# Seven block products at three instead of two of the eight k-tile pairs of each wide FFN panel

## The chip, the cores and the metric

One core of a Trainium2 chip runs the whole program. The metric is the device time of one execution in microseconds (us); of the kernel before, the median of three executions is shown. The engines have names of their own in the rows: PE is TensorE (PEld its weight loads), DVE is VectorE, ACT is ScalarE, POOL is GpSimd, SP is SyncE, which issues the weight loads from memory.

## What is computed

Two transformer-like layers over 256 tokens of width 2048, in float32. Each ends in a feed-forward network (FFN) of width 8192, and only that part is touched:

```python
u = rmsnorm(x, g_mlp) @ w_up                        # 256x2048 @ 2048x8192
return x + jnp.square(jax.nn.relu(u)) @ w_down      # 256x8192 @ 8192x2048
```

The second layer has the same FFN with other weights. All other parts (state space mixer, sparse attention, delta rule) stay as they are.

## The kernel before

**Precision.** Every float32 operand is split in two parts of a shorter format, `hi` (ScalarE, a copy into fp32r) and `lo` (VectorE, operand minus `hi`). A product is three TensorE passes: hi by hi, lo by hi and hi by lo. An activation tile of 128 by 128 is the stationary operand, 512 columns of weights stream past it; each such pass is one matmul instruction at L250.

**Panels.** `ffn` (L369) takes the hidden width in four slices of 2048. A slice has two wide panels up (`up0`, `up1`; 1024 columns of `w_up` each) and two down (`down0`, `down1`; 1024 columns of `w_down` each), so an FFN is the sequence up0, up1, down0, down1, four times. The very last down panel of an FFN goes by the older function `panel` (L192 to L194) instead. There are thus 15 wide panels in each FFN and 30 in all.

**A wide panel** (`wide`, L235) goes over 2048 rows of weights in eight pairs j = 0..7 of k-tiles. For each pair SyncE loads 1 MB into a `wst` buffer (L267; three such buffers). The result is 256 tokens by 1024 columns: four blocks in four PSUM banks.
- An ordinary pair makes two weight halves of 1024 columns with `parts` (`whi` L261 on ScalarE, `wlo` L262 on VectorE) and uses each in 12 matmuls: 24 matmuls.
- At the pairs in `SPAIRS` the 2 by 2 blocks of tokens/k against k/columns are multiplied with seven products instead of eight (P1 to P7, 21 matmuls). For that VectorE makes sums and differences of weight blocks, `t13` (L279, 1024 columns) and `t24` (L282 and L283, 512 columns each), and the splits need seven blocks of 512 columns instead of four: three halves of 1024 and one of 512. P1, P5, P6 and P7 have banks of their own, so a panel holds all eight banks of PSUM.
- `shared` (L302 on) adds the four extra banks up when the panel's last such pair is through: a ScalarE copy (L306) and four VectorE additions (L307 to L310).

**The activation side.** For every pair in `SPAIRS` the activations must also exist as four sums and differences, split in two parts (`sfh`, `sfl`). `a_forms` (L224) makes them: four VectorE operations on 128 columns (L227 to L230) and one split (ScalarE 512 columns, VectorE 512 columns). For the up panels this is done once per FFN in `x_to_act` (L339); for the down panels once per slice in the end of each up panel (L386 on).

**The end of an up panel.** Four additions on VectorE (L376), ReLU and square on ScalarE (L377, L378), then 16 transposes on TensorE (L390) into PSUM banks that the panel has left, then the splits (L170 ScalarE, L172 VectorE) into the tiles `hT`. For a pair in `SPAIRS` the transposed block is first copied to a buffer `ff` (L394) from which both the split and the forms are made. With `SPAIRS = (2, 5)` pair 2 comes from the end of up0 and pair 5 from the end of up1. The end of a down panel is eight additions into the residual (L410, L413).

**Buffers and order.** The tile framework orders the instructions of each engine when the program is built, by the order of the program and by what its own model holds ready, and each engine then runs its list strictly in order. `whi` and `wlo` have four buffers each, so the splits can be four halves ahead of TensorE. The pool `s2` has 16 buffers of 2 KB, `s4` has 17 of 4 KB, of which 8 hold the input of the FFN and 8 the `hT` tiles of the running slice.

Of the kernel before, what the change touches and what calls it, by code (L numbers as in the profile page):

```python
# [12 lines left out]
AF = mybir.ActivationFunctionType  # L13
# [44 lines left out]
def build(ctx, tc, I, out, tap=None, upto=99):  # L58
    nc = tc.nc
    V, S, G, PE = nc.vector, nc.scalar, nc.gpsimd, nc.tensor  # L60
# [17 lines left out]
    def s4(shape, dt=F32, name="s4"):  # L78
        return sb.tile(shape, dt, name=name, tag="s4", bufs=N4)

    def s2(shape, dt=F32, name="s2"):
        return sb.tile(shape, dt, name=name, tag="s2", bufs=N2)
# [7 lines left out]
    def psum(kind, shape):  # L90
        return pp.tile(shape, F32, name=kind, bufs=2)
# [77 lines left out]
    def split(ps, hi, lo, gain=None):  # L169
        S.activation(hi, ps, AF.Copy, scale=1.0 if gain is None else gain)  # L170
        if gain is None:
            V.tensor_tensor(lo, ps, hi.bitcast(F32), op=OP.subtract)  # L172
        else:
            V.scalar_tensor_tensor(lo, ps, gain, hi.bitcast(F32), op0=OP.mult, op1=OP.subtract)

    def quarter(name):
        return s4([128, 4, 256], F32R, name + "h"), s4([128, 4, 256], F32R, name + "l")

    def at_k(act):
        return lambda kt: tuple(a[:, kt % 4, :] for a in act[kt // 4])  # L180
# [37 lines left out]
            mms(*m)  # L218
        return ps

    SPAIRS = (2, 5)
    turn = [0]

    def a_forms(f, forms, j):  # L224

        sf = s2([128, 4, 128], name="sf")
        V.tensor_tensor(sf[:, 0], f[:, 0, 1], f[:, 1, 1], op=OP.add)  # L227
        V.tensor_tensor(sf[:, 2], f[:, 0, 0], f[:, 0, 1], op=OP.subtract)
        V.tensor_tensor(sf[:, 1], sf[:, 0], f[:, 0, 0], op=OP.subtract)
        V.tensor_tensor(sf[:, 3], f[:, 1, 0], sf[:, 1], op=OP.subtract)  # L230
        sh, sl = s2([128, 4, 128], F32R, "sfh"), s2([128, 4, 128], F32R, "sfl")
        split(flat(sf), flat(sh), flat(sl))
        forms[j] = sh, sl

    def wide(w, r0, c0, lhs, forms):  # L235
# [5 lines left out]
        for k, names in zip((ka[0], ka[1], kb[0], kb[1]), (("P2", "P3"), ("P4", "E"), ("P1", "P5"), ("P6", "P7"))):  # L241
            for b in names:
                B[b] = psum(k, [128, 512])
        ns = len(SPAIRS)
        left = {b: 3 * ns + (0 if b in ("P1", "P5", "P6", "P7") else 6 * (8 - ns)) for b in B}
# [19 lines left out]
        for j in range(8):  # L265
            s = stp.tile([128, 2048], F32, name="wst")
            nc.sync.dma_start(s.rearrange("p (k n) -> p k n", k=2),  # L267
                              w[r0 + j * 256:r0 + j * 256 + 256, c0:c0 + 1024].rearrange("(k p) n -> p k n", p=128))
            if j not in SPAIRS:
                for kk in range(2):  # L270
# [68 lines left out]
    def x_to_act(x, q, gain, forms=None, p=0):  # L339

        for k0 in range(0, 4, 2):
            ps = psum("tp", [128, 512]).rearrange("p (k t c) -> p k t c", k=2, t=2)
            for kk in range(2):
                for t in range(2):
                    PE.transpose(ps[:, kk, t, :], x[:, t, (k0 + kk) * 128:(k0 + kk + 1) * 128], ident)  # L345
            if forms is not None and 2 * p + k0 // 2 in SPAIRS:
                f = s2([128, 2, 2, 128], name="ff")
                for kk in range(2):
                    S.activation(f[:, kk], ps[:, kk], AF.Copy, scale=gain[:, k0 + kk:k0 + kk + 1])
                f_to_act(f, q, k0, forms, 2 * p + k0 // 2)  # L350
                continue
            for kk in range(2):
                k = k0 + kk
                split(ps[:, kk].rearrange("p t c -> p (t c)"), q[0][:, k], q[1][:, k], gain[:, k:k + 1])

    def f_to_act(f, q, k0, forms, j):
        fv = f.rearrange("p k t c -> p (k t c)")
        split(fv, flat(q[0][:, k0:k0 + 2]), flat(q[1][:, k0:k0 + 2]))
        a_forms(f, forms, j)

# [5 lines left out]
    def flat(ap):  # L366
        return ap.rearrange("p k c -> p (k c)")

    def ffn(X, act, forms, w_up, w_down, r, after, tail=0):  # L369
        for s_ in range(4):  # L370
            hT, hforms = [], {}
            for P in range(2):
                B, tags = wide(w_up, 0, s_ * 2048 + P * 1024, at_k(act), forms)
                us = {}
                for i, l, part, bank in shared(B):
                    V.tensor_tensor(part, bank, part, op=OP.add)  # L376
                    S.activation(part, part, AF.Relu, scale=r[:, i:i + 1])  # L377
                    S.activation(part, part, AF.Square)  # L378
                    us[i, l] = part
                for l in (1, 0):  # L380
                    q = quarter("hT")
                    p = len(hT)
                    hT.append(q)
                    for k0 in range(0, 4, 2):
                        pt = psum(tags[k0 // 2], [128, 512])
                        pv = pt.rearrange("p (k t c) -> p k t c", k=2, t=2)  # L386
                        for kk in range(2):
                            for t in range(2):
                                c = (k0 + kk) * 128
                                PE.transpose(pv[:, kk, t, :], us[t, l][:, c:c + 128], ident)  # L390
                        j = 2 * p + k0 // 2
                        if j in SPAIRS:
                            f = s2([128, 2, 2, 128], name="ff")
                            S.activation(f.rearrange("p k t c -> p (k t c)"), pt, AF.Copy)  # L394
                            f_to_act(f, q, k0, hforms, j)
                        else:
                            split(pt, flat(q[0][:, k0:k0 + 2]), flat(q[1][:, k0:k0 + 2]))
            for P in range(2):
                if (s_, P) == (3, 1):
                    for p in (2, 3):  # L400
                        ps = panel(w_down, s_ * 2048, 16, p * 512, 512, at_k(hT), tail=tail if p == 3 else 0)
                        for t in range(2):
                            V.tensor_tensor(X[p][:, t], ps[t], X[p][:, t], op=OP.add)
                            after(p, t)
                    continue
                B, _ = wide(w_down, s_ * 2048, P * 1024, at_k(hT), hforms)
                out_ = shared(B)
                for i, l, part, bank in out_:
                    x = X[2 * P + 1 - l][:, i]
                    V.tensor_tensor(x, part, x, op=OP.add)  # L410
                for i, l, part, bank in out_:
                    x = X[2 * P + 1 - l][:, i]
                    V.tensor_tensor(x, bank, x, op=OP.add)  # L413
                if s_ == 3:
                    for p in range(2):
                        for t in range(2):
                            after(p, t)
# [18 lines left out]
    for c0, n in cols(4624, 1104, 3):  # L436
        ps = panel(w_in, 0, 16, c0, n, at_k(xn), before=next_x if r is None else None)
# [49 lines left out]
    ps = psum("tp", [128, 512])  # L487
# [7 lines left out]
    for j in range(0, 8, 2):  # L495
        ps = psum("tp", [128, 512])
# [7 lines left out]
    for t in range(2):  # L504
# [4 lines left out]
        for i in range(4):  # L509
            for half in range(2):  # L510
                hs = slice(half * 64, half * 64 + 64)
                ps = psum("sx", [128, 512])
# [29 lines left out]
    for c0, n in cols(2560, 2064, 5):  # L542
        ps = panel(w_in, 0, 16, c0, n, at_k(xn))
# [28 lines left out]
    ps = psum("sx", [128, 512])  # L572
# [21 lines left out]
    for src, dst, gain, nh in ((lambda t: K1[:, t], [kT], g_k, 4), (lambda t: Q1[t], qT, g_q, 8)):  # L594
        for j in range(0, nh, 2):
            ps = psum("tp", [128, 512])
# [28 lines left out]
    for g in range(4):  # L625
        Ps = []
        for t in range(2):
            nk = 128 * (t + 1)
            ps = psum("sx", [128, 512])
# [7 lines left out]
        ps = psum("tp", [128, 512])  # L637
# [6 lines left out]
        ps = psum("tp", [128, 512])  # L644
# [3 lines left out]
        ps = psum("sx", [128, 512])  # L648
# [5 lines left out]
        k0 = 2 * (g % 2)  # L654
# [41 lines left out]
    for p in range(3):  # L696
        ps = panel(w_in, 0, 16, 1024 + 512 * p, 512, at_k(xn))
# [3 lines left out]
        if p < 2:  # L701
            xsd.append(s4([128, 2, 512], name="xsd"))
            xdt.append(s4([128, 2, 512], name="xdt"))
            for t in range(2):
                pt = to_tokens(xc, t)
# [7 lines left out]
    ps = psum("tp", [128, 512])  # L713
# [4 lines left out]
    for t in range(2):  # L718
        for g in range(2):
            ps = psum("sx", [128, 512])  # L720
# [4 lines left out]
            for q in range(2):  # L725
                ps = psum("sx", [128, 512])
# [11 lines left out]
            for i in range(8):  # L738
                c = i * 64
# [3 lines left out]
            if t == 1:  # L743
                xdd = s2([128, 512], name="xdd")
                V.tensor_tensor(v8(xdd), v8(xdt[g][:, 0]), b3(ds[:, 8 * g:8 * g + 8], 64), op=OP.mult)
                ps = psum("sx", [128, 512])
# [3 lines left out]
                ps = psum("sx", [128, 512])  # L750
# [13 lines left out]
    for g in range(2):  # L764
        ps = panel(w_in, 0, 16, 512 * g, 512, at_k(xn))
# [32 lines left out]
    for p in range(4):  # L798
        ps = panel(I["w_out"][0], 0, 16, p * 512, 512, at_k(mix), order=list(range(8, 16)) + list(range(8)))
# [244 lines left out]
    ps = psum("sx", [128, 512])  # L1044
# [127 lines left out]
    for gi in range(2):  # L1172
        obq = quarter("ob")
        ob.append(obq)
        for t in range(2):
# [9 lines left out]
            pt = hd(to_heads(O))  # L1185
# [4 lines left out]
    ps = psum("sx", [128, 512])  # L1190
# [5 lines left out]
    ps = psum("sx", [128, 512])  # L1196
# [19 lines left out]
    for t in range(2):  # L1216
# [4 lines left out]
        ps = psum("sx", [128, 512])  # L1221
# [22 lines left out]
    for g in range(2):  # L1244
        oq = quarter("oa")
        oa.append(oq)
        for e2 in range(0, 4, 2):
            PT = []
            for br, (kT_, KV) in enumerate(((ksT, KVs), (kwT, KVw))):
                Ps = []  # L1250
                for t in range(2):
                    nk = 128 * (t + 1)
                    ps = psum("sx", [128, 512])
# [8 lines left out]
                ps = psum("tp", [128, 512])  # L1262
# [6 lines left out]
                ps = psum("tp", [128, 512])  # L1269
# [5 lines left out]
            ps = psum("tp", [128, 512])  # L1275
# [6 lines left out]
            ps = psum("sx", [128, 512])  # L1282
# [12 lines left out]
    for which, (o_, w_, mc) in enumerate(((ob, "w_pb_2", 2048), (oa, "w_pa_2", 0))):  # L1295
        for p in range(4):
            ps = panel(w_in2, 0, 16, 6696 + mc + p * 512, 512, at_k(xn))
# [3 lines left out]
            ps = panel(I[w_][0], 0, 8, p * 512, 512, at_k(o_))  # L1301
# [5 lines left out]
            else:  # L1307
# [4 lines left out]
                for k0 in range(0, 4, 2):  # L1312
                    pt = psum("tp", [128, 512])
# [12 lines left out]
    for p in range(4):  # L1326
        ps = panel(I["w_o_2"][0], 0, 16, p * 512, 512, at_k(M))
# [59 lines left out]
```

## Time and profile before

| what | us |
| --- | --- |
| three executions | 2646.22, 2652.0, 2650.08; median 2650.08 |
| the profiled execution | 2654.01, with a span of 2652.2 from first to last instruction |
| granted TensorE clock, share of full speed, mean | 0.997 |
| TensorE busy | 2623.1 (99%) |
| VectorE busy | 1917.3 (72%) |
| ScalarE busy | 1411.5 (53%) |
| memory traffic | 180 GB/s over the span |

The first FFN's wide panels begin at 408.5 us, the second's at 1948.3 us. In this document E is the moment at which the last matmul of a panel is issued and the next panel's first one follows. In the profile's rows a busy matmul counts its own pass through the array, so successive matmuls overlap; the distance from start to start is what one costs.

### The profile page before, as it was taken

What the parts mean: (1) busy time and instruction counts of PE and PEld (TensorE: products, weight loads), DVE (VectorE), ACT (ScalarE), POOL (GpSimd) and SP (SyncE); (2) the same over time, 40 slices, a digit from 0 to 9 for tenths busy, and PEclk for the clock granted to TensorE, in tenths of its full rate; (3) what the DMA queues carried; (4) which work ended last, traced back from release to release, by engine and by line L of the source; (5) the groups of instructions that cost most, each with busy time, mean ns of one, the idle gap of its engine ahead of it and who ended that gap; (6) DMA issues with size and microseconds to landing.
All of it is one profiled execution on the core that took longest, in us unless ns stands there. A gap on an engine that the chain in (4) does not pass through costs nothing.

```text
span 2652.2 us, 32498 instructions
## 1 busy us (share of the span) xinstructions
PE 2623.1 (99%) x12656; PEld 2195.1 (83%) x12656; DVE 1917.3 (72%) x2593; ACT 1411.5 (53%) x1876; POOL 39.2 (1%) x46
## 2 busy tenths in 40 slices
PE   8999999999999999999999999999999999999998
PEld 8998888888887888888888887888888888888887
DVE  5767767787887887676754767455678888888886
ACT  5465455546556556554533554444456455465564
POOL 0000000000000000000100000000000000000000
PEclk9999999999999999999999999999999999999999
DMA  7454555565555555653432743556555555555544
GB/s 237 144 172 159 175 188 182 175 207 191 190 205 176 191 191 191 213 194 127 131 97 86 252 161 113 181 191 212 193 190 176 207 200 183 203 190 191 206 175 175
DMA packets 192153, 478.63 MB, mean 180 GB/s; under 512 B 9128, under 2 KB 50047, under 8 KB 191999
## 3 DMA queue, kind: packets, MB, share of 16 engines
q1 hardware_dynamic: 185840, 467.57, 52.3%
q10 hardware_dynamic: 6158, 8.99, 1.0%
q8 instruction: 99, 1.62, 0.2%
q14 instruction: 56, 0.45, 0.0%
HBM read 472.32 MB, written 4.21 MB: 180 GB/s over the span
## 4 chain that ended last, share of the span: by engine, by line
PE 92%; DMA 3%; DVE 2%; ACT 2%; issue 1%; ACTq 0%; POOL 0%; POOLq 0%; SPq 0%; DVEq 0%
PE mm L250 21%; PE mm L193 13%; PE mm L194 13%; PE mm L192 13%; PE tp L250 11%; PE sx L250 10%; DMA wst<-in_w_down_dram 2%; DVE wlo L262 2%; PE sx L982 1%; ACT whi L261 1%; PE sx L977 1%; PE tp L345 1%; PE mm L390 1%; DMA wst<-in_w_up_dram 1%; PE tp L876 0%
## 5 line engine op out<-in xcount | busy, mean ns | idle before, releaser
L208 DVE TENSOR_TENSOR wlo<-wst,whi 128x1024 fp32r<-128x1024 f32 (+6 forms) x416 | 475.8, 1147 | 321.6 <-ACT whi L207 320.7
L261 ACT ACTIVATE whi<-wst 128x1024 fp32r<-128x1024 f32 x480 | 476.8, 1005 | 379.3 <-PE mm L250 164.1
L207 ACT ACTIVATE whi<-wst 128x1024 fp32r<-128x1024 f32 (+6 forms) x416 | 414.7, 998 | 467.4 <-PE mm L194 437.2
L262 DVE TENSOR_TENSOR wlo<-wst,whi 128x1024 fp32r<-128x1024 f32 x480 | 543.5, 1155 | 140.7 <-ACT whi L261 133.1
L193 PE MATMUL mm<-wlo,x2h 128*128 128x512 f32 (+3 forms) x736 | 279.4, 380 | 0.8 <-DVE wlo L208 0.8
L194 PE MATMUL mm<-whi,x2l 128*128 128x512 f32 (+3 forms) x736 | 279.3, 380 | 0.0
L192 PE MATMUL mm<-whi,x2h 128*128 128x512 f32 (+3 forms) x736 | 279.1, 380 | 0.0
L261 ACT ACTIVATE whi<-t 128x1024 fp32r<-128x1024 f32 x120 | 127.3, 1061 | 150.5 <-PE mm L250 76.8
L262 DVE TENSOR_TENSOR wlo<-t,whi 128x1024 fp32r<-128x1024 f32 x120 | 146.9, 1224 | 80.1 <-ACT whi L261 79.7
L250 PE MATMUL mm<-whi,xnh 128*128 128x512 f32 x432 | 169.0, 391 | 0.0
L250 PE MATMUL mm<-whi,xnl 128*128 128x512 f32 x432 | 168.4, 390 | 0.0
L250 PE MATMUL mm<-wlo,xnh 128*128 128x512 f32 x432 | 168.2, 389 | 0.0
L193 PEld LDWEIGHTS mm<-wlo,x2h 128*128 128x128 f32 x736 | 139.0, 189 | 21.2 <-DVE wlo L208 1.4
L192 PEld LDWEIGHTS mm<-whi,x2h 128*128 128x128 f32 x736 | 139.0, 189 | 20.2 <-issue 1.1
L194 PEld LDWEIGHTS mm<-whi,x2l 128*128 128x128 f32 x736 | 138.9, 189 | 19.9 <-issue 0.9
L192 PE MATMUL mm<-whi,xnh 128*128 128x512 f32 (+3 forms) x416 | 153.0, 369 | 2.0 <-ACT whi L207 1.6
L193 PE MATMUL mm<-wlo,xnh 128*128 128x512 f32 (+3 forms) x416 | 152.2, 366 | 0.0
L194 PE MATMUL mm<-whi,xnl 128*128 128x512 f32 (+3 forms) x416 | 150.9, 366 | 0.1
L250 PE MATMUL mm<-whi,hTh 128*128 128x512 f32 x378 | 148.4, 393 | 0.0
L250 PE MATMUL mm<-wlo,hTh 128*128 128x512 f32 x378 | 147.7, 391 | 0.0
L250 PE MATMUL mm<-whi,hTl 128*128 128x512 f32 x378 | 147.5, 390 | 0.0
L250 PEld LDWEIGHTS mm<-whi,xnl 128*128 128x128 f32 x432 | 81.1, 188 | 17.0
(532 smaller groups left out, 5303.7 us busy)
## 6 DMA issues: line engine op xcount, KB each, us to landing
wst<-in_w_up_dram SPq DMA_DIRECT2D x128, 1024.0 KB, 4.9
wst<-in_w_down_dram SPq DMA_DIRECT2D x128, 1024.0 KB, 5.5
wst<-in_w_in_dram SPq DMA_DIRECT2D x84, 1024.0 KB, 5.0
wst<-in_w_out_dram SPq DMA_DIRECT2D x16, 1024.0 KB, 5.2
wst<-in_w_o_dram SPq DMA_DIRECT2D x16, 1024.0 KB, 5.0
wst<-in_w_in_dram SPq DMA_DIRECT2D x16, 780.0 KB, 4.4
wst<-in_w_in_dram SPq DMA_DIRECT2D x12, 824.0 KB, 4.5
wst<-in_w_in_dram SPq DMA_DIRECT2D x12, 736.0 KB, 6.3
```

The costliest lines, as they stand in the source:

```text
L192: PE.matmul(ps[t][:, :n], xh[:, sl], wa, start=kt == first, stop=False)
L193: PE.matmul(ps[t][:, :n], xh[:, sl], wb, start=False, stop=False)
L194: PE.matmul(ps[t][:, :n], xl[:, sl], wa, start=False, stop=kt == last)
L207: S.activation(a[:, :2 * n], src, AF.Copy)
L208: V.tensor_tensor(b[:, :2 * n], src, a[:, :2 * n].bitcast(F32), op=OP.subtract)
L250: PE.matmul(B[b], x, y, start=left[b] == total[b], stop=left[b] == 1)
L261: S.activation(a[:, :n], src, AF.Copy)
L262: V.tensor_tensor(b[:, :n], src, a[:, :n].bitcast(F32), op=OP.subtract)
L345: PE.transpose(ps[:, kk, t, :], x[:, t, (k0 + kk) * 128:(k0 + kk + 1) * 128], ident)
L390: PE.transpose(pv[:, kk, t, :], us[t, l][:, c:c + 128], ident)
L977: PE.matmul(ps[:, i * 64:(i + 1) * 64].rearrange("p (m b) -> p m b", b=b), N[:, i], half(T[:, i], 0), start=True, stop=True)
L982: PE.matmul(ps[:, i * 64:(i + 1) * 64].rearrange("p (m b) -> p m b", b=b), P[:, i], half(Tt[:, i], 1), start=True, stop=True)
```

## The change

A third pair gets seven products: pairs 2, 4 and 6 instead of 2 and 5. The buffer `ff` and the four sums and differences `sf`, two buffers of 2 KB from `s2` before, now lie together in one buffer of 4 KB from `s4` (the 17th, which the FFN left free), through the new function `two_forms`. In `s2` there are then 12 buffers of `sfh`/`sfl` (three pairs, two sets) beside the four of `shared`: 16 of 16.

```diff
-    SPAIRS = (2, 5)
+    SPAIRS = (2, 4, 6)
     turn = [0]
 
+    def two_forms():
+        f = s4([128, 2, 512], name="ff")
+        return f[:, 0].rearrange("p (k t c) -> p k t c", k=2, t=2), f[:, 1].rearrange("p (f c) -> p f c", f=4)
+
     def a_forms(f, forms, j):
 
-        sf = s2([128, 4, 128], name="sf")
+        sf = f[1]
+        f = f[0]
         V.tensor_tensor(sf[:, 0], f[:, 0, 1], f[:, 1, 1], op=OP.add)
@@ x_to_act
             if forms is not None and 2 * p + k0 // 2 in SPAIRS:
-                f = s2([128, 2, 2, 128], name="ff")
+                f = two_forms()
                 for kk in range(2):
-                    S.activation(f[:, kk], ps[:, kk], AF.Copy, scale=gain[:, k0 + kk:k0 + kk + 1])
+                    S.activation(f[0][:, kk], ps[:, kk], AF.Copy, scale=gain[:, k0 + kk:k0 + kk + 1])
                 f_to_act(f, q, k0, forms, 2 * p + k0 // 2)
@@ f_to_act
-        fv = f.rearrange("p k t c -> p (k t c)")
+        fv = f[0].rearrange("p k t c -> p (k t c)")
@@ ffn
                         if j in SPAIRS:
-                            f = s2([128, 2, 2, 128], name="ff")
-                            S.activation(f.rearrange("p k t c -> p (k t c)"), pt, AF.Copy)
+                            f = two_forms()
+                            S.activation(f[0].rearrange("p k t c -> p (k t c)"), pt, AF.Copy)
                             f_to_act(f, q, k0, hforms, j)
```

## Rows read from the trace of the kernel before

**Rows 1.** The page: span, busy time by engine, chain by engine.
```profile
span 2652.2 us, 32498 instructions
PE 2623.1 (99%) x12656; PEld 2195.1 (83%) x12656; DVE 1917.3 (72%) x2593; ACT 1411.5 (53%) x1876; POOL 39.2 (1%) x46
...
PE 92%; DMA 3%; DVE 2%; ACT 2%; issue 1%; ACTq 0%; POOL 0%; POOLq 0%; SPq 0%; DVEq 0%
```

**Rows 2.** Stretches, line L250 alone: stretch, its length, PE, PEld (instructions), clock.
```profile
1948.00:2600.00 652.00, 637.76 (x2790) 522.48 (x2790) 1.00 0.55 194
717.36:759.52 42.16, 42.16 (x188) 34.93 (x186) 1.00 0.58 201
```

**Rows 3.** Stretches: length, then PE, PEld, DVE, ACT, POOL busy. Sum: four panels.
```profile
671.75:717.36 45.61, 44.36 (x204) 36.48 (x202) 39.95 (x50) 28.26 (x35) 0.00 (x0) 1.00 0.54 179
717.36:759.52 42.16, 42.16 (x188) 34.93 (x186) 34.90 (x39) 20.75 (x21) 0.00 (x0) 1.00 0.58 201
sum 173.91, PE 172.66 PEld 142.94 DVE 142.42 ACT 97.89 POOL 0.00; mean PE 43.16 PEld 35.73 DVE 35.61 ACT 24.47 POOL 0.00
```

**Rows 4.** Waits of TensorE: who waited for whom, total us, times, longest.
```profile
PE tp L390 <- ACT cu L378: 5.3, 4, 1.7
...
PE mm L390 <- ACT cu L378: 4.5, 5, 1.5
```

**Rows 5.** The chain from 660 to 690 us, end of an up1 panel: start, us, what.
```profile
660.56 3.50 DVE wlo L262 x3
...
664.07 7.30 DMA wst<-in_w_down_dram
...
671.39 0.04 DVE t L279
...
672.53 0.70 DVE cp L376
...
677.25 0.33 PE tp L390
...
687.60 0.68 PE tp L250 x3
```

**Rows 6.** Timeline of VectorE, end of an up0 panel: start, us, engine, line.
```profile
625.31 1.23 DVE L279 TENSOR_TENSOR t<-wst 128x1024 f32<-128x1024 f32 x1 [0.47 <-DMA wst<-in_w_up_dram]
626.45 0.69 DVE L376 TENSOR_TENSOR cp<-mm,cp 128x512 f32<-128x512 f32 x1
627.05 1.28 DVE L376 TENSOR_TENSOR cu<-mm,cu 128x512 f32<-128x512 f32 x2
```

**Rows 7.** Timeline of TensorE after that end: the first transposes.
```profile
631.85 0.38 PE L390 MATMUL mm<-idt,cu 128*128 128x128 f32 x2
```

**Rows 8.** Timeline of VectorE at pair 2 of a down panel.
```profile
720.44 1.22 DVE L279 TENSOR_TENSOR t<-wst 128x1024 f32<-128x1024 f32 x1
721.57 1.22 DVE L262 TENSOR_TENSOR wlo<-wst,whi 128x1024 fp32r<-128x1024 f32 x1
722.71 0.69 DVE L282 TENSOR_TENSOR t<-wst,t 128x512 f32<-128x512 f32 x1
723.43 0.69 DVE L283 TENSOR_TENSOR t<-wst,t 128x512 f32<-128x512 f32 x1
724.14 1.23 DVE L262 TENSOR_TENSOR wlo<-t,whi 128x1024 fp32r<-128x1024 f32 x1
726.86 1.23 DVE L262 TENSOR_TENSOR wlo<-t,whi 128x1024 fp32r<-128x1024 f32 x1 [1.49 <-ACT whi L261]
729.16 0.69 DVE L262 TENSOR_TENSOR wlo<-wst,whi 128x512 fp32r<-128x512 f32 x1 [1.08 <-ACT whi L261]
730.94 5.04 DVE L262 TENSOR_TENSOR wlo<-wst,whi 128x1024 fp32r<-128x1024 f32 x4 [1.08 <-ACT whi L261]
```

**Rows 9.** Timelines of ScalarE and VectorE: the forms of one pair, buffer `ff`.
```profile
681.61 0.59 ACT L394 ACTIVATE ff<-sx 128x512 f32<-128x512 f32 x1
683.60 0.29 DVE L227 TENSOR_TENSOR sf<-ff 128x128 f32<-128x128 f32 x1
683.80 0.29 DVE L228 TENSOR_TENSOR sf<-ff 128x128 f32<-128x128 f32 x1
686.74 0.69 DVE L172 TENSOR_TENSOR sfl<-sf,sfh 128x512 fp32r<-128x512 f32 x1
```

## The prediction

> **What bounds the kernel now.** I read the page first: TensorE is busy for 99% of the span and makes up 92% of the chain that ended last [rows 1]. The busy share alone doesn't say that TensorE is the limit, since matmuls overlap in it, so the second view is one wide panel by itself. A down panel lasts 42.16 us and loads 186 stationary tiles, which is the count from the code (six ordinary pairs of 24 and two of 21) [rows 2]. 42.16 / 186 = 0.2267 us from one matmul to the next, and the panel contains nothing else and no idle time: its length is the number of matmuls. 15 such panels of 186 make the 2790 of the second FFN [rows 2], and the first has as many.
>
> The third view is what stands beside TensorE. VectorE is busy for 142.4 of the 173.9 us of four successive panels, 82%, and for 39.95 of 45.61 us (88%) in the panel after an up1 [rows 3]. ScalarE has 97.9 us and is far from a limit.
>
> The fourth is where TensorE does wait in the FFNs: at the first transposes after an up panel, 5.3 + 4.5 = 9.8 us in 9 of the 16 cases [rows 4]. The chain shows how [rows 5]: the last `wlo` of pair 7 ends at 664.05, which frees a `wst` buffer; the load of the next panel's pair 2 into it takes 7.30 us; VectorE's next instruction in its list is the `t13` of that pair, so it stands still until 671.39; only behind that come the additions L376 (672.53), then ScalarE, and the transposes at 677.25. Another case has no wait: there L376 began at 626.45 and the transposes ran at 631.85 [rows 6, 7]. From L376 to transposes the waiting case takes 4.72 us, so the other could have begun at 631.17 and had 0.68 us to spare.
>
> **The change, part by part.**
>
> **1. Matmuls.** One pair per panel goes from 24 to 21. 3 x 30 panels = 90 matmuls of 0.2267 us = 20.4 us, all on the path that sets the end. Each panel becomes 0.68 us shorter (183 matmuls, 41.48 us).
> The Trainium skill (TensorE: Matmul & The Clock Gate, Back-to-back issue gap) gives about 131 ns per matmul of 512 columns for a sustained stream of weight loads and matmuls. By it the saving would be an estimated 90 x 0.131 = 11.8 us. The trace differs with its 226.7 ns over 186 matmuls in a row without idle time, and the sum goes by that.
>
> **2. Weight side on VectorE.** A pair with seven products costs `t13` 1.13 (720.44 to 721.57), `t24` 0.72 + 0.71 (722.71 to 723.43 to 724.14), three halves and a short one [rows 8]. A half costs (3.50 - 1.23) / 2 = 1.13 when three follow one another [rows 5, 8]; a 512-column operation takes 0.60 (626.45 to 627.05) [rows 6]. Sum 1.13 + 1.43 + 3.39 + 0.60 = 6.55 us, against 2.26 for an ordinary pair: +4.29 per panel. ScalarE gets one and a half more copies of a half, about 1.5 us; with 97.9 of 173.9 us busy it hides them.
>
> **3. Activation side.** One more set of forms per slice: four operations of 0.2 (683.60 to 683.80) and a split of 0.6: +1.4 us of VectorE per slice [rows 9], and one set per FFN at its beginning, whose first use is at pair 4 or 6, over 20 us later. Taken at nothing by itself.
> So in four panels VectorE goes from 142.4 to 142.4 + 4 x 4.29 + 1.4 = 161.0 us, and TensorE from 173.9 to 173.9 - 4 x 0.68 = 171.2: 94%. In the panel after up1 it is 39.95 + 5.7 = 45.6 against 44.9, which only fits because the buffers carry work over panel ends. The cover is thin: 10.2 us per four panels.
>
> **4. Crowding on VectorE.** No row shows VectorE at 94%. Below: nothing, since pairs with and without seven products alternate, so 6.55 + 2.26 = 8.8 us of VectorE stand against 45 x 0.2267 = 10.2 of TensorE. Above: today VectorE stands idle 1.49 + 1.08 + 1.08 = 3.65 us at each such pair while ScalarE waits for a free `whi` [rows 8]. Three of these make 10.95 us per panel; the three sets of `t13` and `t24` (2.56 each, 7.7) can be slotted into them, which leaves 3.25 against 10.2 / 4 = 2.55 us to spare. The deficit of 0.7 us on 30 panels is 21 us. Below nothing isn't possible, as nothing is taken off VectorE. I take +5, nearer to the lower end, since the additions at the panel ends can fill the same idle times.
>
> **5. The end of the panel.** The last pair with seven products moves from 5 to 6, so `shared`, which had 48 matmuls of cover (10.9 us), gets 24 and the tail of pair 6, about 6 us, for 4 x 0.6 = 2.4 us of additions. No cost if they keep their place ahead of the next panel's halves.
> The release of pair 7's `wst` moves too. Its second half needs the `whi` buffer of the fourth half before it; that was pair 5's last one, 48 matmuls before E, and is now pair 6's second, 33 matmuls or 7.5 us before E. With a ScalarE and a VectorE operation (about 1.1 + 1.2 us, and 0.2 to start) the release comes at about E - 5.0; now it is at 664.05, E - 7.7. The load for the next pair 2 lands 2.7 us later.
> What that does hangs on the order of VectorE's list. If `t13` stays ahead of L376, nine ends wait 2.7 longer and the seven others 2.7 - 0.7 = 2.0: 9 x 2.7 + 7 x 2.0 = +38 us. If L376 goes first, the late load is covered and the 9.8 us of today can vanish. In the last 7.5 us before E VectorE now has the two halves of pair 7 (2.3), `shared` (2.4), L376 (2.4) and two halves of the next pair 0 (2.3), all earlier in the program than `t13`: 9.4 us, with no idle moment for it to be taken early. I expect L376 first and take half of the gain, -5; both ends, -9.8 and +38, stay.
>
> **6. One buffer for `ff` and `sf`.** After up1 pairs 4 and 6 both need it, where pair 5 alone did. It is held from 681.61 to 687.43, 5.8 us [rows 9], so the second copy comes at about 687 and frees its PSUM bank at 687.6. That bank is wanted by P5 of the next panel's pair 2, which ran at 687.60 [rows 5]: just in time, and 1.25 us late if the transposes' wait vanishes. Between 0 and 8 x 1.3 = 10 us; I count it within the +5 of item 4.
> The Trainium skill (Perfetto Trace Analysis, Optimization Strategy) says that the same gap repeated on the engine that should be full can mean too few buffers. By it there would be eight equal gaps at P5, an estimated 10 us at most by the bound above. No row of before shows one, as two buffers were used there.
>
> Sum: 2654.0 (profiled execution) - 20.4 + 5 - 5 = 2633.6. That execution is 3.9 us above the median of the runs shown, so the median is 2629.7, say 2630.
>
> **The rivals.**
> *A wait in place of the saving (slower).* `t13` stays ahead of L376. For it: it is so in both ends shown [rows 5, 6]. Against it: the crowded list in item 5. It decides from the point where VectorE's list has a free moment before E in which the framework holds the load landed. Time: 2654.0 - 20.4 + 38 - 3.9 = 2668.
> *VectorE becomes the bound (no gain).* The 21 us of item 4 in full: 2654.0 - 20.4 + 21 - 3.9 = 2651. For it: 94% with idle times forced by ScalarE. Against: the panel ends fill some, and four halves of buffer even out the rest.
> *The transposes' wait vanishes and nothing crowds:* 2654.0 - 20.4 - 9.8 - 3.9 = 2620. This is the low end of the forecast's own range.
>
> **How the numbers follow.** My forecast (2630, own range 2618 to 2644) has a chance of 0.68, VectorE as the bound 0.15 (2645 to 2658), the wait at the transposes 0.17 (2660 to 2680). The range of 8 in 10 takes in the first two and leaves the third out: 2616 to 2660. About 0.2% (5.3 us) can be told from no change: faster means under 2644.8. The forecast is faster nearly throughout (0.67), and of the second 0.04: 0.71. Within 0.2% lie 0.09 of the second and 0.01 of the first: 0.10. Slower: 0.17 and 0.02 of the second, 0.19.
>
> **What would show it.** Item 1: 183 weight loads and 41.5 us in a down panel without waits. Items 2 and 3: VectorE at about 161 us in four panels of some 171. Item 4: no waits of L250 for `wlo` or `whi` on TensorE; if they are there and sum to some 20 us, VectorE is the bound. Item 5: on VectorE L376 ahead of L279 after an up panel, and the wait of the transposes under 10 us in total; the reverse order with 40 to 50 us of waits shows the first rival. Item 6: TensorE waiting at P5 for the bank that ACT L394 reads. The prediction is wrong if down panels don't get shorter by 0.7 us, or if the waits at panel ends or within pairs grow by more than 15 us together.

## The result

Six executions of the changed kernel have a median of 2633.53 us (2631.75 to 2636.03), six of the kernel before 2650.26 (2646.22 to 2652.98). The ratio is 0.9939, with a 95% interval of 0.9926 to 0.9952: faster by 0.6%, 16.7 us. The forecast was 2630 within 2616 to 2660.

The page of the changed kernel, its parts on the span, the engines and the chain (L250 is now L255, L261 and L262 are L266 and L267, L376 is L381, the residual additions L410 and L413 are L415 and L418, and `t13` moved from L279 to L284):

```profile
span 2630.4 us, 32664 instructions
PE 2602.5 (99%) x12566; PEld 2171.2 (83%) x12566; DVE 2033.5 (77%) x2791; ACT 1463.4 (56%) x1956; POOL 38.6 (1%) x46
...
PE 90%; DVE 5%; DMA 2%; ACT 1%; issue 1%; ACTq 0%; POOL 0%; POOLq 0%; SPq 0%; DVEq 0%
```

Against [rows 1] TensorE has the forecast 90 matmuls less (12656 to 12566), VectorE 116 us more work, and VectorE's share of the chain grew from 2% to 5%. The next view is four successive panels by stretch, as in [rows 3]: length, then busy time of PE, PEld, DVE, ACT and POOL. The first panel follows a down panel, the next two follow up panels and hold the transposes, the last follows a down panel again.

```profile
580.79:622.82 42.03, 41.78 (x185) 34.27 (x184) 37.72 (x43) 22.34 (x23) 0.00 (x0) 1.00 0.60 201
622.82:666.28 43.46, 43.46 (x200) 35.85 (x199) 39.86 (x50) 29.64 (x37) 0.00 (x0) 1.00 0.59 192
666.28:709.75 43.47, 43.47 (x201) 35.85 (x199) 40.88 (x54) 30.22 (x39) 0.00 (x0) 1.00 0.58 193
709.75:752.53 42.78, 42.14 (x185) 34.11 (x183) 38.84 (x46) 22.10 (x23) 0.00 (x0) 1.00 0.60 199
sum 171.74, PE 170.86 PEld 140.08 DVE 157.31 ACT 104.30 POOL 0.00; mean PE 42.71 PEld 35.02 DVE 39.33 ACT 26.08 POOL 0.00
```

and a down panel of the second FFN by the same view, line L255 alone (PE and PEld):

```profile
2234.88:2276.43 41.55, 41.55 (x185) 34.21 (x184) 1.00 0.59 203
```

The panel after up1, 45.61 us in [rows 3], takes 43.47: more than the 0.68 of three matmuls went. But a panel behind a down panel, which had 42.16 without any idle time, now takes 42.78 as the second down panel of a slice in the first FFN and has idle time (PE busy 42.14); only in the second FFN is that panel at 41.55, next to the expected 41.48. The waits changed places, as TensorE's waits show (who waited for whom, total us, times, longest):

```profile
PE mm L192 <- DVE X L418: 2.6, 1, 2.6
PE tp L255 <- DVE wlo L267: 1.6, 3, 0.7
...
PE tp L255 <- ACT whi L266: 0.7, 3, 0.2
PE mm L255 <- ACT whi L266: 0.7, 3, 0.2
PE mm L255 <- DVE wlo L267: 0.6, 3, 0.2
```

The 9.8 us at the transposes [rows 4] are gone altogether. In their place stand waits for weight halves inside panels, and one of 2.6 us behind the last wide panel of the first FFN.

Where the time went, from the first matmul of one panel to the first of the next, in the profiled executions (us):

| stretch | before | changed |
| --- | --- | --- |
| first FFN, 15 wide panels and the wait behind them | 660.7 | 647.7 |
| second FFN, 15 wide panels | 651.4 | 641.3 |
| from there to the last matmul | 43.7 | 45.6 |
| all else | 896.4 | 895.8 |
| span | 2652.2 | 2630.4 |

Fifteen wide panels without any wait would take 648.1 us before (a first one of 43.2, eight of 43.99 with transposes, six of 42.16) and 637.9 after. So the kernel before held 12.6 + 3.3 = 15.9 us of waits above that, the changed one 9.8 + 3.4 and 1.9 at the end, 15.1. The sum is -20.4 for the matmuls, -15.9 for the old waits, +15.1 for new ones and -0.6 for all else: -21.8.

Not all of the 15.9 is waiting. One panel of the kernel before took 47.73 us at a mean granted clock of 0.96:

```profile
847.44:895.17 47.73, 45.99 (x203) 37.84 (x202) 40.20 (x50) 28.25 (x35) 0.00 (x0) 0.96 0.53 171
```

There TensorE waited 1.74 us for the transposes' input (to 853.42), and from 854.1 to 857.5 its granted clock was 0.5, 1.2 instead of 2.4 GHz. 3.4 us at half speed lose some 1.7 us. The profiled execution of before was 3.8 us above the median; if that lies in these waits and in the clock, the old waits are about 12 us in the median.

### The profile page after: what moved, and what is told of

It is laid out like the page before. It is cut to its first block, busy times and chain, and to the rows that moved or that the text cites. A ratio compares the mean times of both kernels' runs of the same rounds, so it can differ in the third digit from the quotient of the medians.

```text
span 2630.4 us, 32664 instructions
## 1 busy us (share of the span) xinstructions
PE 2602.5 (99%) x12566; PEld 2171.2 (83%) x12566; DVE 2033.5 (77%) x2791; ACT 1463.4 (56%) x1956; POOL 38.6 (1%) x46
## 4 chain that ended last, share of the span: by engine, by line
PE 90%; DVE 5%; DMA 2%; ACT 1%; issue 1%; ACTq 0%; POOL 0%; POOLq 0%; SPq 0%; DVEq 0%
PE mm L255 21%; PE mm L193 13%; PE mm L194 13%; PE mm L192 13%; PE tp L255 10%; PE sx L255 9%; DVE wlo L267 3%; DMA wst<-in_w_down_dram 1%; PE sx L987 1%; PE sx L982 1%; PE tp L350 1%; ACT whi L266 1%; PE mm L395 1%; PE tp L881 0%; DVE wlo L208 0%
## 5 line engine op out<-in xcount | busy, mean ns | idle before, releaser
L266 ACT ACTIVATE whi<-wst 128x1024 fp32r<-128x1024 f32 x480 | 465.8, 979 | 275.8 <-PE mm L255 116.0
L267 DVE TENSOR_TENSOR wlo<-wst,whi 128x1024 fp32r<-128x1024 f32 x480 | 527.9, 1119 | 58.5 <-ACT whi L266 55.9
L266 ACT ACTIVATE whi<-t 128x1024 fp32r<-128x1024 f32 x180 | 190.2, 1057 | 214.2 <-DVE t L288 89.2
L192 PE MATMUL mm<-whi,x2h 128*128 128x512 f32 (+3 forms) x736 | 279.0, 379 | 0.0
L267 DVE TENSOR_TENSOR wlo<-t,whi 128x1024 fp32r<-128x1024 f32 x180 | 219.6, 1220 | 41.3 <-ACT whi L266 39.4
L192 PEld LDWEIGHTS mm<-whi,x2h 128*128 128x128 f32 x736 | 138.9, 189 | 20.3 <-issue 1.1
L192 PE MATMUL mm<-whi,xnh 128*128 128x512 f32 (+3 forms) x416 | 152.6, 368 | 2.0 <-ACT whi L207 1.6
L255 PE MATMUL mm<-wlo,xnh 128*128 128x512 f32 x392 | 153.0, 390 | 0.0
L255 PE MATMUL mm<-whi,xnl 128*128 128x512 f32 x392 | 152.7, 390 | 0.0
L255 PE MATMUL mm<-whi,xnh 128*128 128x512 f32 x392 | 151.9, 391 | 0.7 <-ACT whi L266 0.7
L255 PE MATMUL mm<-wlo,hTh 128*128 128x512 f32 x343 | 133.9, 390 | 0.0
L255 PE MATMUL mm<-whi,hTl 128*128 128x512 f32 x343 | 133.6, 389 | 0.0
L255 PE MATMUL mm<-whi,hTh 128*128 128x512 f32 x343 | 132.0, 390 | 0.0
L284 DVE TENSOR_TENSOR t<-wst 128x1024 f32<-128x1024 f32 x90 | 109.7, 1219 | 13.4 <-DMA wst<-in_w_down_dram 10.9
```

Of the source, the lines that this page charges most:

```text
L192: PE.matmul(ps[t][:, :n], xh[:, sl], wa, start=kt == first, stop=False)
L255: PE.matmul(B[b], x, y, start=left[b] == total[b], stop=left[b] == 1)
L266: S.activation(a[:, :n], src, AF.Copy)
L267: V.tensor_tensor(b[:, :n], src, a[:, :n].bitcast(F32), op=OP.subtract)
L284: V.tensor_tensor(t13, s.rearrange("p (k l n) -> p k l n", k=2, l=2)[:, :, 0], s[:, :1024].rearrange("p (l n) -> p l n", l=2)[:, ::-1], op ...
```

## The experiments

**Three matmuls fewer and nothing else.** Of the kernel before, three matmuls per panel left out at pair 7:

```diff
...
-                        product(b, xh[:, h], xl[:, h], *wl[l])
+                        if (j, kk) == (7, 1) and b != "E":
+                            mm(b, xh[:, h], wl[l][0])
+                            mm(b, xh[:, h], wl[l][1])
+                        else:
+                            product(b, xh[:, h], xl[:, h], *wl[l])
```

> The kernel before with three matmuls per wide panel left out: the low part of the activations against the high part of the weights, for three of the four blocks of the last k-tile; nothing else is changed, VectorE and the order at the panel ends stay. It measures what 90 matmuls are worth by themselves. Theory (TensorE at 0.2267 us per matmul is the limit everywhere): 20.4 us less, 2630, with the waits at the transposes as they were, some 10 us. Rival (VectorE or the loads follow close behind): less than 15 us.

It measured 2617.3 us, ratio 0.9874 (0.9860 to 0.9887): 32.6 us less, more than either theory. A panel behind a down panel is at 41.48, as worked out, and one behind an up panel at 43.44, without waits; the wide panels of its two FFNs take 638.9 and 639.1 us, next to the 637.9 without any wait:

```profile
620.14:663.58 43.44, 43.44 (x201) 35.93 (x199) 36.36 (x44) 28.12 (x37) 0.00 (x0) 1.00 0.57 193
707.01:748.49 41.48, 41.48 (x184) 34.38 (x183) 34.59 (x39) 20.74 (x21) 0.00 (x0) 1.00 0.61 203
```

The 12.2 us beyond 20.4 are what the old waits come to in the median, and VectorE's timeline at the end of an up panel (next panel from 620.14) shows why they went although nothing was moved by hand:

```profile
618.75 0.69 DVE L382 TENSOR_TENSOR cp<-mm,cp 128x512 f32<-128x512 f32 x1 [0.85 <-PE mm L252]
619.36 1.28 DVE L382 TENSOR_TENSOR cu<-mm,cu 128x512 f32<-128x512 f32 x2
620.55 0.68 DVE L382 TENSOR_TENSOR cv<-mm,cv 128x512 f32<-128x512 f32 x1
621.15 1.22 DVE L264 TENSOR_TENSOR wlo<-wst,whi 128x1024 fp32r<-128x1024 f32 x1
622.29 1.22 DVE L285 TENSOR_TENSOR t<-wst 128x1024 f32<-128x1024 f32 x1
```

The additions (L382 here) come ahead of `t13` (L285), the other way round than in [rows 6]: the framework's order turned with three matmuls less. This kernel is the yardstick for the change: 20.4 us of matmuls and 12.2 of waits are to be had, 32.6; the change got 16.7 and so gave back 15.9 of it.

**Two pairs, at 2 and 6.** `SPAIRS = (2, 6)` in the changed kernel.

> Two pairs with seven products as before, but at 2 and 6 instead of 2 and 5; buffers as in the changed kernel. No matmul less than before. Theory: the last such pair at 6 crowds VectorE's list before the panel's end, so that the additions of an up panel come ahead of the next t13 and the transposes wait no longer: 10 to 13 us less than before, 2638 to 2641, and no wait of the transposes beyond 0.3 us each. Rival (the vanished wait belongs to the third pair's greater load on VectorE, not to the place of the last one): t13 first as before, and a load that lands 2.7 us later: 2650 to 2690.

It measured 2649.9 us, ratio 0.9995 (0.9986 to 1.0004): no change. The theory's 10 to 13 us less didn't come; the rival's range begins right here, but its mechanism (`t13` first) isn't what the trace shows. The mechanism of the theory is there (the additions come ahead of `t13` in all sixteen ends), its gain isn't. The panel behind an up panel shows no wait (44.16 us; 43.99 was the shortest before), but the panel behind a down panel went from 42.16 to 42.70:

```profile
669.54:713.70 44.16, 44.16 (x204) 36.43 (x202) 36.75 (x46) 28.05 (x35) 0.00 (x0) 1.00 0.59 190
713.70:756.40 42.70, 42.45 (x188) 34.85 (x186) 34.50 (x39) 20.75 (x21) 0.00 (x0) 1.00 0.60 199
```

VectorE's timeline at that panel's beginning (713.70):

```profile
713.76 2.48 DVE L418 TENSOR_TENSOR X<-mm,X 128x512 f32<-128x512 f32 x4
716.16 3.48 DVE L267 TENSOR_TENSOR wlo<-wst,whi 128x1024 fp32r<-128x1024 f32 x3
```

TensorE wants the second half of pair 0 at 713.70 + 12 x 0.2267 = 716.42, and VectorE begins with it at 716.16, because the residual additions stand in front of it. Twelve panels behind a down panel pay 0.54 each (6.5 us), the sixteen behind up panels 0.16 (2.6, the transposes lie less well between the matmuls), the two FFN ends 0.9 and 1.4: 11.4 us, about as much as was gained. And VectorE isn't full there, with 343.8 of 420 us (82%):

```profile
580.00:1000.00 420.00, 418.77 (x1879) 344.63 (x1878) 343.78 (x395) 236.50 (x272) 0.00 (x0) 1.00 0.58 195
```

So moving the last pair from 5 to 6 takes the old waits away and puts as many new ones in place, and the third pair by itself then brings 2649.9 - 2633.5 = 16.4 of its 20.4 us.

**The buffers alone.** `SPAIRS = (2, 5)` in the changed kernel.

> Pairs 2 and 5 as before, only ff and the sums in one 4 KB buffer of the other pool. Theory: with one such pair per up panel the buffer is never wanted twice at once, so no change: within 4 us of before. Rival (the move of the buffers by itself changes the order or adds a wait): more than 5 us either way.

2650.5 us, ratio 0.9999 (0.9990 to 1.0008), as expected: the single buffer for `ff` and the sums costs nothing by itself.

**What the old wait was.** Two kernels from the one before: smaller pools, and with them a fourth buffer for loads.

```diff
-    NP, N4, N2, N1 = 7, 17, 16, 5
+    NP, N4, N2, N1 = 7, 16, 14, 5
...
-    stp = ctx.enter_context(tc.tile_pool(name="stp", bufs=3))
+    stp = ctx.enter_context(tc.tile_pool(name="stp", bufs=4))
```

> The kernel before with 16 instead of 17 buffers of 4 KB and 14 instead of 16 of 2 KB, which is what its FFNs use; it stands beside the next kernel, which needs that room. All theories: the FFNs' time as before, the whole within 6 us of before.

> The kernel before with the smaller pools and four instead of three buffers for the loads of weights, so that pair 2 of the next panel is loaded some 5 us earlier. Theory (what makes the transposes wait is VectorE standing at t13 for a load that came late, in front of the additions): the waits of the transposes vanish, 8 to 13 us less than small_pools, 2637 to 2643. Rival (the transposes wait because VectorE or ScalarE has too much to do at the panel's end): the same as small_pools.

small_pools took 2658.9 us, 7.9 above before (outside the 6 us; its FFNs begin 9 us later, so the smaller pools cost in what lies ahead), four_loads 2648.8, 10.1 less than small_pools, inside the theory's 8 to 13. The theory's 2637 to 2643 was missed by what small_pools lost. In TensorE's waits small_pools has two lines at the transposes

```profile
PE tp L390 <- ACT cu L378: 5.7, 5, 1.5
...
PE mm L390 <- ACT cu L378: 2.6, 4, 1.3
```

and four_loads one:

```profile
PE mm L390 <- ACT cu L378: 0.4, 1, 0.4
```

In four_loads `t13` still begins before the additions in all sixteen ends, but it now waits little for its load; in all `t13` waits 9.8 us for loads, against 25.2 in small_pools. At one end (additions L376):

```profile
673.59 1.22 DVE L279 TENSOR_TENSOR t<-wst 128x1024 f32<-128x1024 f32 x1 [0.54 <-DMA wst<-in_w_down_dram]
...
676.47 0.69 DVE L376 TENSOR_TENSOR cp<-tp,cp 128x512 f32<-128x512 f32 x1
```

So the wait came from the load of pair 2, at which VectorE stood in front of the additions. It wasn't a shortage of work time at the panel's end.

**More work for VectorE.** In the changed kernel the second `t24` operation is issued twice (t24_half), or both are; the edit of t24_twice:

```diff
             V.tensor_tensor(t24[:, 0], s[:, 1024:1536], t13[:, 0], op=OP.subtract)
             V.tensor_tensor(t24[:, 1], s[:, 1536:], t24[:, 0], op=OP.subtract)
+            V.tensor_tensor(t24[:, 0], s[:, 1024:1536], t13[:, 0], op=OP.subtract)
+            V.tensor_tensor(t24[:, 1], s[:, 1536:], t24[:, 0], op=OP.subtract)
```

> The changed kernel with both t24 operations issued twice, with the same values: 2.9 us more VectorE work at each pair with seven products in latency (1.4 in occupancy), 3 x 1.4 = 4.3 us per panel. VectorE would stand at about 157 + 17 = 174 us against 171.7 of four panels, so it becomes the limit. Theory (the changed kernel is close below the point where VectorE is the bound): at least 2.8 us per four panels, 7.5 x 2.8 = 21 us, with forced idle times up to 60: 2655 to 2695. Rival (there is still room): under 10 us more than the changed kernel.

> The changed kernel with the second t24 operation issued twice: 0.7 us more VectorE work at each pair with seven products, 2.1 per panel, 166 of 171.7 us in four panels, still below full. Theory (the changed kernel lies at the bend: with every operation issued twice it lost 89 us for 129 us of added VectorE work): 15 to 50 us more than the changed kernel. Rival (the bend lies higher, and only a VectorE beyond full costs time): under 8 us more.

t24_twice took 2722.8 us, 89 more than the changed kernel and more than the 60 at which the theory ended; t24_half 2671.9, 38 more, inside its 15 to 50. The rival in each (room left) falls. For 30 x 2.1 = 63 us of work added the time grew by 38, for 129 by 89: of each microsecond on VectorE 0.6 to 0.7 came through. The stretch from 580 to 1000 us, all in the first FFN (columns as above), for t24_half and for t24_twice:

```profile
580.00:1000.00 420.00, 410.98 (x1817) 330.83 (x1816) 390.43 (x474) 240.63 (x291) 0.00 (x0) 1.00 0.55 189
```
```profile
580.00:1000.00 420.00, 404.60 (x1741) 317.46 (x1740) 392.41 (x478) 231.13 (x273) 0.00 (x0) 1.00 0.53 183
```

VectorE is busy for 390.4 and 392.4 of 420 us, 93% with either. In the profile of t24_twice TensorE's granted clock also fell to 0.5 for 3.4 us four times in the wide panels (at 514, 698, 1067 and 2084 us), each time behind waits of TensorE that sum to 1.9 or 2.0 us; that is some 7 of its 89 us.

**Less work for VectorE.** Four of the eight residual additions of a down panel go to GpSimd behind VectorE's other four (pool_parts), or are left out (no_parts):

```diff
-                for i, l, part, bank in out_:
-                    x = X[2 * P + 1 - l][:, i]
-                    V.tensor_tensor(x, part, x, op=OP.add)
                 for i, l, part, bank in out_:
                     x = X[2 * P + 1 - l][:, i]
                     V.tensor_tensor(x, bank, x, op=OP.add)
+                for i, l, part, bank in out_:          # pool_parts alone
+                    x = X[2 * P + 1 - l][:, i]
+                    G.tensor_tensor(x, part, x, op=OP.add)
```

> The changed kernel with four of the eight residual additions of a down panel on GpSimd, behind VectorE's four of the banks: 2.4 us per down panel off VectorE, TensorE's work as it is. Theory (what the changed kernel lacks to a pure saving of matmuls, 16 us against the kernel with three fewer, are places where VectorE is late): the waits after down panels go, 5 to 12 us less than the changed kernel, 2621 to 2629. Rival (those waits come from loads and from the order of TensorE's list, or GpSimd slows VectorE as much as it helps): within 4 us of it or slower.

> The changed kernel with four residual additions per down panel left out (those of the shared sums; the outcome lacks them), and nothing on GpSimd: 2.4 us less VectorE per down panel, as in pool_parts, without a second engine at work beside it. Theory (VectorE is late in the changed kernel, and in pool_parts its operations were slowed while GpSimd worked, 2.3 instead of 1.2 us): 5 to 15 us less than the changed kernel, 2618 to 2628. Rival (the order alone made pool_parts slower): the same as pool_parts or the changed kernel, 2633 to 2645.

pool_parts took 2644.1 us, ratio 0.9971 (0.9959 to 0.9983) to before: 10.5 more than the changed kernel, against the theory. The timelines of VectorE and GpSimd behind a down panel (711.03) show how, first VectorE's:

```profile
711.32 1.88 DVE L415 TENSOR_TENSOR X<-mm,X 128x512 f32<-128x512 f32 x3
713.11 3.71 DVE L267 TENSOR_TENSOR wlo<-wst,whi 128x1024 fp32r<-128x1024 f32 x2
716.74 2.31 DVE L284 TENSOR_TENSOR t<-wst 128x1024 f32<-128x1024 f32 x1
```

and GpSimd's:

```profile
712.20 3.54 POOL L418 TENSOR_TENSOR X<-cu,X 128x512 f32<-128x512 f32 x2
715.70 2.27 POOL L418 TENSOR_TENSOR X<-cv,X 128x512 f32<-128x512 f32 x1
```

While GpSimd adds, `t13` takes 2.31 us instead of 1.22 and two halves 3.71 instead of 2.35: VectorE loses about what it was spared, and loses it where it is already late. Another 3.3 us are two waits of transposes behind the first FFN for GpSimd's own additions. Without GpSimd, no_parts, whose outcome lacks those four sums, took 2619.1 us, ratio 0.9884 (0.9868 to 0.9901): 14.5 less than the changed kernel, inside the theory's range. Its two FFNs have 639.2 and 639.4 us and TensorE waits nowhere in a wide panel:

```profile
580.00:1000.00 420.00, 420.00 (x1890) 347.08 (x1889) 377.04 (x439) 259.00 (x302) 0.00 (x0) 1.00 0.60 197
```

377.0 of 420 us are 89.8%; the changed kernel in the same stretch has

```profile
580.00:1000.00 420.00, 417.90 (x1872) 342.81 (x1871) 384.72 (x455) 254.33 (x298) 0.00 (x0) 1.00 0.59 196
```

384.7 us, 91.6%. So 2.4 us less of VectorE's work per down panel are worth nearly all that the change gave back. The share of busy time alone doesn't set the cost, though. The same stretch of the second FFN, for the changed kernel and for t24_half:

```profile
2100.00:2520.00 420.00, 419.27 (x1883) 345.07 (x1882) 388.56 (x461) 256.36 (x300) 0.00 (x0) 1.00 0.57 197
```
```profile
2100.00:2520.00 420.00, 412.92 (x1814) 331.36 (x1813) 388.61 (x467) 237.86 (x282) 0.00 (x0) 1.00 0.54 192
```

Both have 92.5%, more than the changed kernel's first FFN; yet the changed kernel has 3.4 us of waits in its second FFN, t24_half 24.6 (662.5 us against 637.9). And pairs_2_6 paid 11.4 us at 82%. What no_parts leaves out are additions that stand in front of the next panel's first halves. Whether their place or the sheer amount of work counts for more, these runs don't separate.

**Two pairs in the last wide panel.** It is the one in front of the 2.6 us wait for `X L418`.

```diff
+            hpairs = SPAIRS if s_ < 3 else (2, 4)
...
-                B, _ = wide(w_down, s_ * 2048, P * 1024, at_k(hT), hforms)
+                B, _ = wide(w_down, s_ * 2048, P * 1024, at_k(hT), hforms, hpairs)
```

> The changed kernel, but with pairs 2 and 4 alone in the last wide panel of each FFN (and no third forms for it). That panel is the only one with a wait of its first successor: 2.7 us in the first FFN and a tail that is 1.9 us longer in the second. Theory (these are VectorE being late with shared and the additions behind a pair 6): 4.6 - 2 x 0.7 = 3.2 us less than the changed kernel, 2630. Rival (they belong to the older function that follows): 1.4 us more.

2627.7 us, ratio 0.9916 (0.9902 to 0.9931): 5.8 less than the changed kernel, where 3.2 were expected; the line `PE mm L192 <- DVE X L418` is gone from TensorE's waits. It is faster than both kernels. The profiled executions differ by 5.3 us, and 2.5 of these lie outside the wide panels and the end: the changed kernel's had a granted clock of 0.5 for 3.4 us from 1553.2 us, between the FFNs, which is some 1.7 us, and the one of last_two had not. Whether the edit has to do with that isn't shown.

## Why the prediction was right, step by step

The time came out 3.5 us above the forecast, by the mechanism that was forecast, but two terms of the sum were each some 10 us too small in the profiled executions, with opposite signs. That they cancelled was luck.

**1, matmuls: right.** 90 fewer, 20.4 us; where no wait interferes a down panel is 41.48 (three_fewer) or 41.55 us (second FFN). The 0.2267 us hold for 183 matmuls as for 186, so the Trainium skill's 131 ns for such a stream (TensorE: Matmul & The Clock Gate, Back-to-back issue gap) isn't what this kernel shows.

**2 and 3, VectorE's work: somewhat high.** 161.0 us for four panels was expected, 157.3 measured. The step that failed is the addition of 4.29 us per panel to a busy time in which not all operations count alike: an operation with idle time behind it counts 1.22 or 1.23, one in a row 1.13, and in the changed kernel more of them stand in a row. In the four panels 56 operations had idle time behind them before and 29 have it now; 27 x 0.09 = 2.4 us of the 3.7.

**4, crowding: mis-sized.** +5 was taken from bounds of 0 and 21; it is 15.1 us. "The additions at the panel ends can fill the same idle times" failed: the ends are where VectorE is late. Its timeline near the beginning of a panel behind a down panel (580.79):

```profile
582.11 1.28 DVE L418 TENSOR_TENSOR X<-sx,X 128x512 f32<-128x512 f32 x2
583.30 3.49 DVE L267 TENSOR_TENSOR wlo<-wst,whi 128x1024 fp32r<-128x1024 f32 x3
```

and TensorE's there:

```profile
584.20 0.39 PE L255 MATMUL mm<-whi,xnh 128*128 128x512 f32 x1
584.83 0.50 PE L255 MATMUL tp<-whi,xnh 128*128 128x512 f32 x1 [0.25 <-ACT whi L266]
```

From 584.20 to 584.83 are 0.63 us for one matmul, 0.41 too much. The trace puts this wait down to a `whi` of pair 2, which ScalarE began when TensorE had freed its buffer:

```profile
583.71 1.06 ACT L266 ACTIVATE whi<-wst 128x1024 fp32r<-128x1024 f32 x1 [1.66 <-PE mm L255]
```

In TensorE's list a matmul with this `whi` stands ahead of the first with the second half's `wlo` (585.16), the one that VectorE began at 583.30 only. That the list was made so because of the late `wlo` is likely but not shown; in no_parts, where VectorE has less to do there, the wait is gone. Six panels of this kind have 0.54 us each of it, 3.2 us. Three down panels of the first FFN have 1.3 to 1.5 each, 4.2 us, within the panel; the end of the first FFN has 2.7, the end of the second 1.9, and the sixteen panels with transposes 0.16 each, 2.6, as in pairs_2_6. The sum is 14.6 of the 15.1. In those three down panels VectorE stands at `t13` of the pairs 4 and 6 for their loads, 2.6 to 2.8 us in each. The chain at the first of the two, for the panel from 709.75 (start, us, what; entries of 0.02 us left out), leads back to the residual additions:

```profile
712.22 1.88 DVE X L418 x3
714.10 2.28 DVE wlo L267 x2
716.39 5.62 DMA wst<-in_w_down_dram
722.04 0.70 DVE t L284
```

The additions delay the two halves whose end frees a `wst` buffer, the load into it takes 5.62 us, and `t13` waits 1.06 for it. In the second FFN `t13` of pair 4 waits 0.5 to 0.6 us in these panels, and they are at 41.5 to 41.6 us.

Item 4 had weighed VectorE against a full 100% and looked for the cost inside the pairs. The runs show the cost at 92%, and at 82% in pairs_2_6, where the panels meet: the rival "VectorE becomes the bound" was the right worry, but the waits lie where the residual additions stand in VectorE's list, and how much of them comes from its load as a whole stays open.

The prediction's own signs come out mixed. Down panels were to get shorter by 0.7 us: those behind a down panel got longer by 0.6 to 0.8 in the first FFN and shorter by 0.6 in the second. No waits of L250 for `wlo` or `whi` were to be seen: L255 has 3.6 us of them. And the new waits, 15.1 us, stand at the 15 that were to show it wrong, though the old 15.9 went at the same time.

**5, the transposes: right in kind, mis-sized.** L376 was expected ahead of `t13` for want of an idle moment, and so it is, in all sixteen ends; the first of the additions (L381 now) begins 0.60 us before the panel's end at 666.28 and `t13` comes after it all:

```profile
665.68 0.68 DVE L381 TENSOR_TENSOR cp<-tp,cp 128x512 f32<-128x512 f32 x1
...
668.07 2.35 DVE L267 TENSOR_TENSOR wlo<-wst,whi 128x1024 fp32r<-128x1024 f32 x2
670.34 1.22 DVE L284 TENSOR_TENSOR t<-wst 128x1024 f32<-128x1024 f32 x1
```

Half of 9.8 us was taken; all of it went. The bound itself was low: the wait lines of [rows 4] count TensorE's own idle time, while the panels' lengths held 15.9 us in that execution, some 1.7 of it by the clock, and some 12 in the median. The first rival (`t13` first, 2668) didn't occur; what it would have cost isn't measured, but four_loads bears out the chain on which it rests.

**6, one buffer: right.** Nothing by itself (buf_alone), and TensorE's waits have no line for P5's bank. The Trainium skill's rule that a repeated gap can mean too few buffers (Perfetto Trace Analysis, Optimization Strategy) does fit the kernel before, where a fourth buffer for loads took the repeated gap at the transposes away; three_fewer and pairs_2_6 lost it without one, by the order alone.

## What to carry to other kernels

Where TensorE is the limit, each matmul saved is worth its distance to the next; what the saving asks of a neighbour engine can cost before that engine is full: here 15 us with VectorE at 92%, and 0.6 to 0.7 us for each one added to that. How full the engine is doesn't tell it by itself: pairs_2_6 paid 11 us at 82%. Look at the boundaries between stages first: that is where the neighbour's extra work (sums, residuals) meets the next stage's first operands. And before pricing a wait, look whether an instruction that waits for a load stands in front of urgent work in an engine's list: such a wait can go, or come, with an edit elsewhere that turns the order.

## What the runs showed of the hardware

VectorE slowed by a factor of up to 1.9 while GpSimd worked on other data in SBUF: 2.31 us against 1.22 for the same subtraction of 128x1024 (pool_parts). Operations with both operands in SBUF were slowed, the 27 splits of 128x1024 that ran mostly beside GpSimd to 1.46 to 2.32 us; the 42 additions of 128x512 to the residual from a PSUM bank that ran mostly beside it kept their 0.68 us. The Trainium skill (Perfetto Trace Analysis, Optimizing Scalar/DVE Operations) says that the two share a read port of SBUF and that moving work between them might not help; the trace agrees for operands in SBUF, and with it the kernel was 10.5 us slower.

TensorE's granted clock fell from 1.0 to 0.5 for 3.4 us behind single waits or pairs of waits of some 1.7 to 2.0 us in otherwise full stretches: once in the profile of before (at 854.1 us), four times in that of t24_twice. Successive matmuls then started 0.43 us apart instead of 0.23, so that such a wait cost nearly twice its length. It doesn't follow every such wait: the one of 2.56 us in the changed kernel, which ended at 1056.01, brought no fall.
